# A longer written-out ring of gathers on GpSimd, and a wait ahead of its drain, in a masked-cumulative-sum kernel

## The chip, the cores and the metric

The kernel runs on one core of a Trainium2 chip. The metric is the device time of one execution in microseconds; a kernel's time is the median of several executions.

## What is computed

For each of 8 sequences the reference sums the rows of x from position 0 up to the middle of the sequence's length, and multiplies the sum by w:

```python
mask = (pos < lengths[:, None, None]).astype(np.float32)
cs = np.cumsum(x * mask, axis=1)
midpoints = (lengths // 2).clip(0)
mid_features = cs[b_idx, midpoints, :]
return np.matmul(mid_features[:, None, :], w).squeeze(1)
```

x is 8 x 8192 x 512 in float32, w is 512 x 512. Since the midpoint is always inside the length, only the rows 0 to length // 2 of each sequence matter. How many these are depends on the lengths, which are data.

## The kernel before

The kernel reads only the rows that count. It takes the sum as a matmul: rows of x stand on the 128 partitions, and a small matrix of zeros and ones (`ww`, one column for each sequence) is the stationary side, so PE adds up rows into `s_ps`.

Rows come in three ways. The rows 64 to 255 of each sequence (the front) are fetched by SP at once (L467). Rows beyond 256 are gathered by GpSimd: one indirect DMA brings 128 units of 8 rows (128 x 16 KB, 2 MB) into one of R = 3 slots of `xt` (`fetch`, L227 to L231). The first 64 rows of each sequence (`xb`) and w (`wt`) are fetched last, in plain DMAs of GpSimd, behind all gathers (L256 to L263). w comes in four pieces with a semaphore each, `s_w[0]` to `s_w[3]`.

The number of gathers is known only on the chip. DVE works it out and leaves it in `count`; each engine loads it into a register and loops. The order of the work is written out by hand, with semaphores:

- GpSimd makes three opening gathers (L236 to L248), then a ring of further ones. A turn of the ring waits for `s_now`, which tells that the indices of the slot have been written, issues the gather, and takes `s_now` down again (L250 to L252). When no gather is left it goes to `gp_end` (L255), issues the DMAs for xb and w, drains (L264), waits for both stores of the output (`s_out`, L265) and leaves.
- SP waits for each gather's landing (`s_full`) and for its weights (`s_wr`), and passes this on to PE as `s_rdy` (`relay`, L149).
- PE multiplies a slot's 8 rows of each partition (L395) and says `s_done`.
- ACT then copies the next indices to `now` (L185, which raises `s_now`) and the next weights to `ww` (L188).

At the end PE adds the xb rows into `d_ps`, combines both sums with a folding matrix (`mf_ps`, L446 and L449), and multiplies by the pieces of w (`o_ps`, L459); DVE and ACT copy the result out, and SP and ACT store a half each (L207).

The function `ring` (L123) writes the loop of an engine. Each turn has a compare that leaves the ring, the body, and a branch to the next turn; the last turn takes the turns off the register `left` and goes back to the first. It is used by SP, ACT and GpSimd, with as many turns written out as `xt` has slots.

Of the kernel before, what the change touches and what calls it, by code (L numbers as in the profile page):

```python
# [15 lines left out]
def kernel(  # L16
# [22 lines left out]
    R = 3  # L39
# [20 lines left out]
    def sem(name):  # L60
        return tc.alloc_semaphore(name)
# [46 lines left out]
    s_w = [sem(f"w{k}") for k in range(4)]  # L108
# [11 lines left out]
    def weights_by_rows(at, n):  # L120
        return ww[:, at * B:(at + n) * B].rearrange("p (u b) -> p u b", b=B)

    def ring(eng, name, left, body):  # L123
        for s in range(R):
            with nc.body(f"{name}_0_{s}", valid_engines=[eng.engine]):
                eng.br_cmp(left, s, f"{name}_1_{s}", f"{name}_end", "IS_GT")  # L126
            with nc.body(f"{name}_1_{s}", valid_engines=[eng.engine]):
                body(s)
                if s == R - 1:
                    eng.reg_sub(left, left, R)  # L130
                eng.br(f"{name}_0_{(s + 1) % R}")


    def sync(sp):
        left = sp.alloc_register("left_sp")
        full = sp.alloc_register("full_sp")
        have = sp.alloc_register("have_sp")
        sp.reg_mov(full, 16)
        sp.reg_mov(have, 1)
        sp.wait_ge(s_dve, marks["count"])  # L140
        sp.load(left, count[:])
        sp.wait_ge(s_dve, marks["front"])
        sp.wait_ge(s_zero, 3)
        for f in range(PARTS):
            sp.wait_ge(s_front[f], 16)
            sp.sem_inc(s_rdy, 1)
        sp.br("sy_0_0")

        def relay(s):  # L149
            sp.wait_ge(s_wr, have)  # L150
            sp.wait_ge(s_full[s], full)
            sp.sem_inc(s_rdy, 1)
            sp.reg_add(have, have, 1)
            if s == R - 1:
                sp.reg_add(full, full, 16)

        ring(sp, "sy", left, relay)
        with nc.body("sy_end", valid_engines=[sp.engine]):
            sp.wait_ge(s_dve, marks["out0"])
            sp.wait_ge(s_act, 3)  # L160
            store(sp, 0)
            sp.br(END)


    def scalar(act):
# [16 lines left out]
        def weigh(s):  # L182
# [7 lines left out]
            act.reg_add(turn, turn, 1)  # L190

        ring(act, "ac", left, weigh)
        with nc.body("ac_end", valid_engines=[act.engine]):
            act.wait_ge(s_pe, 2)
# [15 lines left out]
    def gpsimd(pool):  # L210
        pool.iota(v_i[:], pattern=[[P * U, C], [1, U]], base=HEAD, channel_multiplier=0)
        pool.iota(r_i[:, FU:], pattern=[[2, BU], [-(BU // 2), FB]], base=0,
                  channel_multiplier=BU // 2).then_inc(s_pool, 1)
        pool.wait_ge(s_pool, 1)
        for k in range(4):
            pool.iota(at_i[32 * k:32 * k + 32], pattern=[[P, C]],
                      base=64 * (k % 2) + 8 * (k // 2) + 63 * 8 * k,
                      channel_multiplier=16).then_inc(s_pool, 1)
        pool.tensor_scalar(out=row[:, 2 * B + 2:], in0=lens[:, ::2], scalar1=0.5, scalar2=0.25,
                           op0=ALU.mult, op1=ALU.add)._wait_ge(s_len, 16).then_inc(s_pool, 1)  # L220
        pool.wait_ge(s_pool, 6)
        pool.iota(r_i[:, :FU], pattern=[[2, FU], [-(FU // 2), FB]], base=2 * TOP,
                  channel_multiplier=FU // 2)
        pool.iota(fold_i[:], pattern=[[-32, 2], [-1, B]], base=P, channel_multiplier=1,
                  ).then_inc(s_pool, 1)

        def fetch(to, units, at, n, full):  # L227
            return pool.indirect_dma_start(  # L228
                out=to, out_offset=None, in_=units,
                in_offset=bass.IndirectOffsetOnAxis(ap=at, axis=0),  # L230
                bounds_check=n - 1, oob_is_err=False).then_inc(full, 16)  # L231

        left = pool.alloc_register("left_pool")
        pool.wait_ge(s_dve, marks["idx"])
        pool.br("gp_b_0")
        for c in range(R):  # L236
            if c > 0:
                with nc.body(f"gp_a_{c}", valid_engines=[pool.engine]):
                    pool.br_cmp(left, c, f"gp_b_{c}", "gp_end", "IS_GT")
            with nc.body(f"gp_b_{c}", valid_engines=[pool.engine]):  # L240
                got = fetch(xt[:, c], xu, now[:, c:c + 1], B * UB, s_full[c])
                if c > 0:
                    got._wait_ge(s_done, c)
                if c == 0:
                    pool.load(left, count[:])  # L245
                if c == R - 1:
                    pool.reg_sub(left, left, R)
                pool.br(f"gp_a_{c + 1}" if c + 1 < R else "gp_0_0")  # L248

        def gather(s):  # L250
            fetch(xt[:, s], xu, now[:, s:s + 1], B * UB, s_full[s])._wait_ge(s_now, 1)
            pool.sem_inc(s_now, -1)  # L252

        ring(pool, "gp", left, gather)
        with nc.body("gp_end", valid_engines=[pool.engine]):  # L255
            for f in range(PARTS):  # L256
                pool.dma_start(out=xb[:, f], in_=x[FB * f:FB * (f + 1), :TOP].rearrange(  # L257
                    "b (q u) d -> q b (u d)", u=BU)).then_inc(s_back[f], 16)
            pool.dma_start(out=wt[:, :2], in_=w[HALVES[0]].rearrange("(p k) d -> p k d", k=2),
                           ).then_inc(s_w[0], 16)  # L260
            pool.dma_start(out=wt[:, 2], in_=w[QUARTERS[2]]).then_inc(s_w[1], 16)
            for g, at in enumerate(HALVES):
                pool.dma_start(out=wt[:, 3, at], in_=w[QUARTERS[3], at]).then_inc(s_w[2 + g], 16)  # L263
            pool.drain()  # L264
            pool.wait_ge(s_out, 32)  # L265
            pool.br(END)
# [126 lines left out]
    def tensor(pe):  # L393
# [40 lines left out]
        with nc.body("pe_end", valid_engines=[pe.engine]):  # L434
# [17 lines left out]
            for k in range(KC):  # L452
# [10 lines left out]

    programs = [(nc.vector, vector, "dv"), (nc.sync, sync, "sy"), (nc.scalar, scalar, "ac"),
                (nc.gpsimd, gpsimd, "gp")]
    for f in range(PARTS):
        nc.sync.dma_start(out=xt[:, f + 1, :FU * D], in_=x[FB * f:FB * (f + 1), TOP:HEAD].rearrange(  # L467
            "b (q u) d -> q b (u d)", u=FU)).then_inc(s_front[f], 16)
    nc.scalar.dma_start(out=lens[:], in_=lens_words).then_inc(s_len, 16)
    left = nc.tensor.alloc_register("left_pe")  # L470
# [37 lines left out]
```

## Time and profile before

| what | value |
|---|---|
| median of 5 runs | 82.94 us (82.58 to 83.58) |
| the profiled execution, its own time | 82.64 us |
| its span, from the first to the last instruction | 80.5 us |
| mean granted TensorE clock | 0.992 |
| busy: PE / POOL / DVE / ACT | 59.3 / 19.9 / 11.8 / 9.7 us |
| read from HBM | 32.51 MB, 404 GB/s over the span |
| gathers | 13, each 4.9 us after the one before in the middle of the span, landing 11.8 us after its issue (median) |

Times in the profile are microseconds from the first instruction. PE is TensorE's matmuls, PEld its weight loads, DVE VectorE, ACT ScalarE, POOL GpSimd, SP SyncE; a "q" behind a name (POOLq, SPq) is the engine's sequencer, which does waits, branches, register work and drains, and isn't counted as busy. PE's busy time holds matmuls whose result isn't used (`idle`, L399), which fill its waits. "issue" in the chain is time in which the engine waited for nothing that the profile shows, here mostly a semaphore wait at the sequencer.

### The profile page before, as it was taken

What the parts mean: (1) busy time and instruction counts of PE and PEld (TensorE: products, weight loads), DVE (VectorE), ACT (ScalarE), POOL (GpSimd) and SP (SyncE); (2) the same over time, 40 slices, a digit from 0 to 9 for tenths busy, and PEclk for the clock granted to TensorE, in tenths of its full rate; (3) what the DMA queues carried; (4) which work ended last, traced back from release to release, by engine and by line L of the source; (5) the groups of instructions that cost most, each with busy time, mean ns of one, the idle gap of its engine ahead of it and who ended that gap; (6) DMA issues with size and microseconds to landing.
All of it is one profiled execution on the core that took longest, in us unless ns stands there. A gap on an engine that the chain in (4) does not pass through costs nothing.

```text
span 80.5 us, 1176 instructions
## 1 busy us (share of the span) xinstructions
PE 59.3 (74%) x360; PEld 14.1 (17%) x360; DVE 11.8 (15%) x43; ACT 9.7 (12%) x31; POOL 19.9 (25%) x32
## 2 busy tenths in 40 slices
PE   0599979996593967939489493975939679399940
PEld 0212202120110202112020110201102021112820
DVE  0799300990000000000000000000000000003130
ACT  2971000102010010201001020010100100000220
POOL 5432050844022040310404004040220793000000
PEclk9999999999999999999999999999999999999996
DMA  0899999999999999999999999999999999999700
GB/s 0 342 427 403 452 427 407 440 432 432 399 423 472 399 407 472 415 415 472 415 407 448 440 407 415 464 423 399 448 448 407 423 456 415 399 383 407 269 0 8
DMA packets 2803, 31.23 MB, mean 388 GB/s; under 512 B 434, under 2 KB 450, under 8 KB 962
## 3 DMA queue, kind: packets, MB, share of 16 engines
q0 software_dynamic: 2480, 28.05, 82.4%
q1 hardware_dynamic: 304, 3.15, 9.5%
q8 instruction: 1, 0.02, 0.1%
q10 hardware_dynamic: 18, 0.01, 0.0%
HBM read 32.51 MB, written 0.02 MB: 404 GB/s over the span
## 4 chain that ended last, share of the span: by engine, by line
issue 59%; POOL 14%; DMA 14%; PE 5%; DVE 2%; POOLq 2%; ACTq 0%; SPq 0%
POOL xt L228 14%; DMA xb<-in_x_dram 12%; DMA lens<-in_lengths_dram 1%; PE mf_ps L446 1%; PE o_ps L395 1%; PE d_ps L395 1%; PE bc_ps L408 1%; DVE o_sb L276 1%; POOL xb L257 1%; POOLq L245 1%; PE mf_ps L449 1%; POOLq L228 0%; DVE row L276 0%; POOLq L126 0%; DVE ge L276 0%
## 5 line engine op out<-in xcount | busy, mean ns | idle before, releaser
L395 PE MATMUL s_ps<-xt,ww 128*8 128x512 f32 x240 | 29.3, 594 | 15.0 <-PEq L415 15.0
L401 PE MATMUL idle_ps<-ones 128*4 128x512 f32 x58 | 29.2, 630 | 0.0
L228 POOL DMA_INDIRECT xt<-in_x_dram,now x13 | 14.8, 1135 | 45.9 <-POOLq L252 36.9
L395 PEld LDWEIGHTS s_ps<-xt,ww 128*8 128x8 f32 x240 | 5.8, 88 | 37.9 <-issue 37.8
L276 DVE COPY s_sb<-s_ps 128x256 f32<-128x256 f32 x2 | 0.8, 420 | 55.4 <-PE s_ps L395 55.4
L401 PEld LDWEIGHTS idle_ps<-ones 128*4 128x4 f32 x58 | 5.1, 90 | 20.4 <-issue 20.4
L185 ACT COPY now<-idx 128x1 int32 x10 | 1.9, 191 | 44.2 <-PE s_ps L395 44.2
L276 DVE TENSOR_TENSOR early<-v_f,ends 128x192 f32<-128x192 f32 (+1 forms) x2 | 2.4, 1192 | 5.4 <-PE s_ps L395 5.4
L408 PE MATMUL bc_ps<-row,ones 1*128 1x26 f32 x2 | 0.6, 398 | 2.9 <-DVE p L276 2.9
L188 ACT COPY ww<-wc 128x64 f32 x10 | 2.4, 244 | 0.1
L276 DVE TENSOR_TENSOR wc<-early,ge 128x192 f32<-128x192 f32 (+1 forms) x2 | 2.4, 1192 | 0.1
L166 ACT ACTIVATE xt<-xt 128x2048 uint32<-128x2048 uint32 x1 | 1.9, 1909 | 0.0
L196 ACT COPY d_sb<-d_ps 128x128 f32<-128x128 f32 x2 | 0.4, 269 | 12.1 <-PE d_ps L395 12.1
L178 ACT COPY ww<-wc 128x64 f32<-128x64 f32 x3 | 0.7, 244 | 8.1 <-PE s_ps L395 6.7
L166 ACT ACT_TABLE_LOAD x1 | 1.3, 1283 | 1.5 <-SPq L52 1.5
L395 PE MATMUL d_ps<-xb,ww 128*8 128x256 f32 x16 | 1.3, 388 | 0.1
L446 PE MATMUL mf_ps<-fold,s_sb 128*128 128x8 f32 x8 | 1.3, 265 | 0.0
L257 POOL DMA_DIRECT2D xb<-in_x_dram x2 | 1.2, 614 | 0.0
L263 POOL DMA_DIRECT2D wt<-in_w_dram x2 | 1.2, 647 | 0.0
L446 PEld LDWEIGHTS mf_ps<-fold,s_sb 128*128 128x128 f32 x8 | 1.1, 196 | 0.5 <-DVE s_sb L276 0.5
L395 PE MATMUL o_ps<-wt,mf_sb 128*8 128x128 f32 x32 | 1.1, 273 | 0.0
L408 PEld LDWEIGHTS bc_ps<-row,ones 1*128 1x128 f32 x2 | 0.5, 306 | 2.9 <-DVE p L276 2.9
(47 smaller groups left out, 14.1 us busy)
## 6 DMA issues: line engine op xcount, KB each, us to landing
xt<-in_x_dram SPq DMA_DIRECT2D x2, 1536.0 KB, 8.2
xb<-in_x_dram POOLq DMA_DIRECT2D x2, 512.0 KB, 9.4
wt<-in_w_dram POOLq DMA_DIRECT2D x1, 512.0 KB, 10.5
wt<-in_w_dram POOLq DMA_DIRECT2D x1, 256.0 KB, 10.7
wt<-in_w_dram POOLq DMA_DIRECT2D x2, 128.0 KB, 10.4
xt<-in_x_dram,now POOLq DMA_INDIRECT x13, 11.8
lens<-in_lengths_dram ACTq DMA_DIRECT2D x1, 0.1 KB
out_dram<-o_sb SPq DMA_DIRECT2D x1, 8.0 KB
```

What stands on the lines that cost most here:

```text
L166: act.memzero(xt[:, 1:, FU * D:]).then_inc(s_zero, 1)
L185: act.copy(out=now[:, s:s + 1], in_=idx[:, bass.ds(c, 1)]).then_inc(s_now, 1)
L188: act.copy(out=weights_of(s), in_=wc[:, bass.ds(c, 1)].rearrange("p c e -> p (c e)"),).then_inc(s_wr, 1)
L228: return pool.indirect_dma_start(out=to, out_offset=None, in_=units, in_offset=bass.IndirectOffsetOnAxis(ap=at, axis=0), bounds_check=n - ...
L245: pool.load(left, count[:])
L257: pool.dma_start(out=xb[:, f], in_=x[FB * f:FB * (f + 1), :TOP].rearrange("b (q u) d -> q b (u d)", u=BU)).then_inc(s_back[f], 16)
L263: pool.dma_start(out=wt[:, 3, at], in_=w[QUARTERS[3], at]).then_inc(s_w[2 + g], 16)
L276: do(*args, **kw).then_inc(s_dve, 1)
L395: return pe.matmul(to[32 * j:32 * j + weights.shape[1], :rows.shape[1]], lhsT=weights, rhs=rows, start=start, stop=False, skip_group_check ...
L401: pe.matmul(idle_ps[:FB], lhsT=ones[:, :FB], rhs=ones[:, :1].to_broadcast((P, D)), start=True, stop=True, skip_group_check=True)
L408: pe.matmul(bc_ps[:, :3 * B + 2], lhsT=ones[:1], rhs=row[:], start=True, stop=True,)._wait_ge(s_dve, marks["row"]).then_inc(s_pe, 1)
L446: pe.matmul(mf_ps[i][:, B * (k % 2):B * (k % 2 + 1)], lhsT=s_sb[:, QUARTERS[k]], rhs=fold[:], start=(k % 2 == 0), stop=False, skip_group_c ...
```

## The change

The ring gets a parameter for the number of turns that are written out. GpSimd's ring is written out for 2R = 6 turns; the slot of a turn is its number modulo 3. SP's and ACT's rings keep three turns. Behind the last DMA of w a wait for `s_w[3]`, the semaphore of w's last piece, is put ahead of the drain.

```diff
-    def ring(eng, name, left, body):
-        for s in range(R):
+    def ring(eng, name, left, body, turns=R):
+        for s in range(turns):
             with nc.body(f"{name}_0_{s}", valid_engines=[eng.engine]):
                 eng.br_cmp(left, s, f"{name}_1_{s}", f"{name}_end", "IS_GT")
             with nc.body(f"{name}_1_{s}", valid_engines=[eng.engine]):
-                body(s)
-                if s == R - 1:
-                    eng.reg_sub(left, left, R)
-                eng.br(f"{name}_0_{(s + 1) % R}")
+                body(s % R)
+                if s == turns - 1:
+                    eng.reg_sub(left, left, turns)
+                eng.br(f"{name}_0_{(s + 1) % turns}")
...
-        ring(pool, "gp", left, gather)
+        ring(pool, "gp", left, gather, 2 * R)
...
                 pool.dma_start(out=wt[:, 3, at], in_=w[QUARTERS[3], at]).then_inc(s_w[2 + g], 16)
+            pool.wait_ge(s_w[3], 16)
             pool.drain()
             pool.wait_ge(s_out, 32)
```

In the built program GpSimd has 84 instructions instead of 69. The wait for `s_w[3]` is carried by the drain itself. A plain turn's branch to the next turn falls away in both kernels, since the next turn follows it; only the last turn's branch, back to the first, is left.

## The prediction

> **What bounds the kernel now.** I read the page first (spans and slices), then the busy time by stage, then the chain that ended last, then the groups of single source lines of GpSimd. The slices of the page:
>
> ```profile
> span 80.5 us, 1176 instructions
> ...
> POOL 5432050844022040310404004040220793000000
> ...
> DMA  0899999999999999999999999999999999999700
> ```
>
> DMA is full from the second slice to slice 37, GpSimd (POOL) mostly idle. The busy time by stage (columns: window, its length, then busy time of PE, PEld, DVE, ACT, POOL, granted clock, DMA share, GB/s) says the same in numbers:
>
> ```profile
> 20.00:64.00 44.00, 32.39 (x180) 6.50 (x180) 0.00 (x0) 3.56 (x18) 9.07 (x10) 1.00 1.01 430
> 64.00:76.30 12.30, 9.97 (x84) 3.36 (x88) 0.93 (x3) 0.43 (x2) 3.12 (x6) 1.00 0.96 389
> 76.30:80.50 4.20, 0.99 (x32) 0.70 (x32) 0.74 (x3) 0.52 (x2) 0.00 (x0) 0.85 0.02 4
> ```
>
> From 20 to 64 us all 16 DMA engines are taken (share 1.01) at 430 GB/s, while GpSimd works 9.07 of 44 us. So the middle is set by bytes, not by who issues them. One gather of 2 MB takes 4.9 us at that rate, and the gathers follow each other at just 4.9 us. The end of the chain, in order of time (start, length, what):
>
> ```profile
> 62.81 0.98 POOL xt L228
> 63.79 0.56 POOL xb L257
> 64.36 9.77 DMA xb<-in_x_dram
> 74.12 0.04 issue
> 74.17 0.64 PE d_ps L395 x8
> ...
> 76.30 1.00 PE o_ps L395 x32
> 77.30 0.02 issue
> 77.32 0.28 DVE o_sb L276
> 77.60 0.03 issue
> 77.63 0.29 DVE o_sb L276
> ```
>
> The last piece of x (xb) lands at 74.1 because it stands behind the gathers; then PE, copies and the two stores follow. GpSimd's drain is not in it. Three lines of GpSimd alone (sequencer operation, count, ns min/median/max, first and last start):
>
> ```profile
> L264 POOLq DRAIN  x1: 11997/11997/11997, 65.6 to 65.6; - x1
> L266 POOLq COMPARE_BRANCH  x1: 42/42/42, 79.4 to 79.4; - x1
> L228 POOL DMA_INDIRECT xt<-in_x_dram,now x13: 984/984/2657, 5.3 to 62.8; - x13
> ```
>
> The drain runs from 65.6 to 77.6. GpSimd then waits for the two stores until 79.4. There are 13 gathers: 3 of the opening and 10 of the ring.
>
> **Part 1, the ring for six turns.** Ten ring gathers make three jumps back now (after turns 3, 6, 9) and one then (after turn 6). A jump turn shows what is saved. In the chain GpSimd's s_now decrement (L252) is at 28.32, then L130 and L131 (36 and 38 ns), the next compare, and the address move of the next gather (L228) at 28.70: 0.38 us. In a plain turn L252 is at 33.22 and the move at 33.37: 0.15 us. So a jump costs 0.23 us, two fewer save 0.46 us of sequencer time. None of it is on the path: the gather of the turn has already gone to the engine (28.55 in the jump turn, 0.23 us after L252; 18.67 after 18.44 in a plain turn, the same 0.23), and after the bookkeeping the sequencer waits 4.49 us for the next index ("28.73 4.49 issue"). That wait is the cover; a delay longer than it would still have to outlast the transfers queued in front. A gather lands 11.8 us after its issue, of which 4.9 are its own bytes, about 1.0 its issue (984 ns) and about 1.2 the latency of a small transfer (that of lens, in the chain): 11.8 - 4.9 - 1.0 - 1.2 = 4.7 us may be lost before the DMA engines run dry. Value taken: 0. What it adds is 15 instructions (69 to 84 on GpSimd by the instruction order): code that may cross a block. That is the rival below.
>
> [...] The row of this trace:
>
> ```profile
> q8 instruction: 1, 0.02, 0.1%
> ```
>
> One block was fetched in the whole execution: 0.1% of 16 engines' 80.5 us, about 1.3 us of one DMA engine (its packet in the trace: from 75.9, 1.1 us). The row doesn't tell whose it is. At 75.9 PE starts on its last stretch (o_ps), and PE's code is the longest by far (its matmuls are written out), so I take it as PE's, which this change leaves where it is. By the row the change costs 0. [...]
>
> **Part 2, the drain waits for the last piece of w.** Queued behind it on GpSimd are only the drain, the wait for both stores and the final branch; the transfers of xb and w are all issued before it, so SP's and ACT's queues and every transfer keep their times. The last w piece is issued at 66.5 and lands 10.3 us later, at about 76.8. Then the drain runs. [...] How long is it if it starts at 76.8? From below: other drains of this trace take nothing that a view lists as busy, so 0. From above: 77.6 less the end of the last issue (65.95 + 1.18 = 67.1), 10.4 us, if its time were fixed. It ended 0.8 us after the last landing, so I take it as waiting for the transfers, with 0.8 us left: end at 77.6 as before. Cover: until 79.4 GpSimd would wait for the stores anyway, so up to 79.4 - 76.8 = 2.6 us cost nothing. Value taken: 0. A gain is bounded too: nothing waits for the drain but the end of the program, which the stores set.
>
> **Sum.** 0 + 0 against the profiled execution: 82.64 us, span 80.5 and 2.1 around it. The median of the five runs, 82.94, is 0.3 above; the forecast for the median is 82.9.
>
> **Rivals.**
> 1. A code block boundary falls into the ring (slower). GpSimd stops after a gather until a block has come. If the block's fetch stands behind the gathers already queued, it comes after about 11.8 + 1.1 = 12.9 us from that gather's issue. The next gather would have been issued 4.9 us after it, so it is 8.0 late; 4.7 of it are covered by the queue, 3.3 are idle DMA: 82.9 + 3.3 = 86.2. It decides from 4.7 us of lateness on; a fetch that overtakes the data (1.1 us) is hidden in the 3.9 us for which GpSimd is idle in each turn. For it: GpSimd's drain ends 0.5 us after that one fetched block, so the block might be GpSimd's, asked for at 65.6 and queued behind data for 10 us. Against: no gather of the trace shows such a gap, and an execution of only 84 instructions needn't cross a block.
> 2. The drain has work of its own per transfer that now starts late (slower). The third gather's issue took 2.66 us against 0.98; if those 1.7 us are the clearing of old transfers and several are due at the drain, it takes 3.5 to 5 us and ends at 80.3 to 81.8, 0.9 to 2.4 us after 79.4: 83.8 to 85.3. With the fixed 10.4 us it would be 82.9 + 7.8 = 90.7. Against: it ended soon after the last landing.
> 3. The fetched block is GpSimd's and leaves the tail (faster). It holds one DMA engine for 1.1 us among the last pieces. Where it stands in front of xb or w, all of PE's end waits: at most 82.9 - 1.1 = 81.8. Against: here o_ps starts at 76.2 and runs 1.06 us without a gap, so the block cost nothing.
> 4. It does nothing that can be seen: the forecast itself.
>
> **How the numbers follow.** No effect 0.50 (82.3 to 83.5, own range); rival 1 0.17 (85.5 to 88); rival 2 0.13 (83.8 to 85.3, little beyond); rival 3 0.20 (81.8 to 82.1). 1% (0.83 us) is about what a measurement of this kernel can tell from no change. So faster 0.20, within 1% 0.50, slower 0.30. The range leaves out the most of rival 3 and the upper half of rival 1: 82.0 to 86.5.
>
> **What would show it.** Part 1 right: gathers still every 4.9 us, DMA share 1.00 from 20 to 64 us, L131 on GpSimd once instead of three times. Part 2 right: a drain of 0.1 to 0.8 us at about 76.8, the last branch of GpSimd still at 79.4. Wrong: one gather issued 8 us late and a slice with DMA below 9 (rival 1); the final branch right behind a long drain (rival 2); the instruction packet moved and xb or o_ps earlier (rival 3).

## The result, and the profile after

The changed kernel takes 83.09 us (median of 42 executions), the one before 83.02 (79 executions). The ratio is 1.0014, its 95% interval 1.0003 to 1.0024: slower by about 0.12 us. That is inside the range of 82.3 to 83.5 us given for "no effect", but it is a small loss and not nothing. The profiled execution took 83.23 us, with a span of 81.1.

What part 1 promised is there. The busy time by stage of the changed kernel, with the columns as before:

```profile
20.00:64.00 44.00, 32.39 (x180) 6.51 (x180) 0.00 (x0) 3.56 (x18) 8.93 (x10) 1.00 1.01 429
```

DMA is as full as before (share 1.01 in both), and GpSimd makes one jump back in its ring instead of three (the source line of the jump, one row for each sequencer; before, GpSimd's row has x3):

```profile
L131 SPq COMPARE_BRANCH  x4: 37/38/38, 26.0 to 70.0; - x4
L131 ACTq COMPARE_BRANCH  x3: 38/38/38, 28.5 to 57.8; - x3
L131 POOLq COMPARE_BRANCH  x1: 38/38/38, 43.3 to 43.3; - x1
```

The chain that ended last takes the same steps with the same lengths:

```profile
64.50 9.78 DMA xb<-in_x_dram
74.28 0.04 issue
74.33 0.64 PE d_ps L396 x8
...
77.48 0.28 DVE o_sb L277
77.75 0.03 issue
77.79 0.29 DVE o_sb L277
```

xb takes 9.78 us to land against 9.77, and from its landing to the last copy there are 3.80 us in both. The chain ends there, but the span doesn't. Behind it stands the closing barrier, in which GpSimd releases the other engines (their steps start 0.04 to 0.06 us after its second semaphore step, at 79.84 to 79.86 us before and at 80.38 to 80.40 after), and it shows only when its source line is asked for. First the kernel before, then the one after (operation, count, ns, start of the first and the last):

```profile
L503 POOLq DRAIN  x3: 34/47/103, 79.6 to 80.2; - x3
L503 SPq EVENT_SEMAPHORE  x2: 17/17/17, 79.8 to 80.4; - x2
```

```profile
L504 POOLq DRAIN  x3: 34/40/146, 79.8 to 80.8; - x3
L504 SPq EVENT_SEMAPHORE  x2: 17/17/17, 80.4 to 81.0; - x2
```

Before, SP passes the barrier 0.2 us after GpSimd's first drain in it; after, 0.6 us. In the instruction records the place is a single step of GpSimd: its two semaphore steps behind that drain start 0.08 us apart before (79.72 and 79.80) and 0.46 us apart after (79.88 and 80.34). The other engines' own drains in the barrier take what they took (SP's 7 ns, ACT's and PE's 8, DVE's 10, in both). (The two profiled spans differ by 0.59 us. About 0.17 of it is there already when GpSimd's last wait ends, 79.36 us before and 79.53 after; since the mean spans below differ by 0.38, I take this part as scatter.) The DMA queues of the changed kernel have a row more than those of the kernel before:

```profile
q8 instruction: 1, 0.02, 0.1%
q14 instruction: 1, 0.01, 0.0%
```

The new packet is 8192 bytes of code, at 81.02 us, 0.7 us after the stalled step. The 16 KB on q8 is still there, at 76.0 us. GpSimd's drain ahead of the barrier, which now waits for w, and the branch behind it, which waits for the stores:

```profile
L265 POOLq DRAIN  x1: 1624/1624/1624, 76.9 to 76.9; - x1
```

```profile
L267 POOLq COMPARE_BRANCH  x1: 43/43/43, 79.5 to 79.5; - x1
```

The drain runs from 76.9 to 78.5, and the branch that waits for the stores is still the later one.

So two numbers have to be put together: a step in the span that costs 0.38 us more, and a time that grew by only 0.12.

### The profile page after: what moved, and what is told of

Read it like the earlier page. It is cut to its first block, busy times and chain, and to the rows that moved or that the text cites. A ratio compares the mean times of both kernels' runs of the same rounds, so it can differ in the third digit from the quotient of the medians.

```text
span 81.1 us, 1172 instructions
## 1 busy us (share of the span) xinstructions
PE 59.7 (74%) x360; PEld 14.1 (17%) x360; DVE 11.8 (15%) x43; ACT 9.7 (12%) x31; POOL 19.9 (25%) x32
## 4 chain that ended last, share of the span: by engine, by line
issue 57%; POOL 16%; DMA 14%; PE 5%; DVE 2%; POOLq 2%; ACTq 0%; SPq 0%
POOL xt L228 16%; DMA xb<-in_x_dram 12%; DMA lens<-in_lengths_dram 1%; PE mf_ps L447 1%; PE o_ps L396 1%; PE d_ps L396 1%; PE bc_ps L409 1%; DVE o_sb L277 1%; POOL xb L257 1%; POOLq L245 1%; PE mf_ps L450 1%; POOLq L228 0%; POOLq L126 0%; DVE row L277 0%; DVE z L277 0%
## 5 line engine op out<-in xcount | busy, mean ns | idle before, releaser
L228 POOL DMA_INDIRECT xt<-in_x_dram,now x13 | 14.7, 1134 | 46.1 <-POOLq L252 37.1
## 6 DMA issues: line engine op xcount, KB each, us to landing
wt<-in_w_dram POOLq DMA_DIRECT2D x1, 512.0 KB, 10.5
wt<-in_w_dram POOLq DMA_DIRECT2D x2, 128.0 KB, 10.4
```

What stands on the lines that cost most here:

```text
L228: return pool.indirect_dma_start(out=to, out_offset=None, in_=units, in_offset=bass.IndirectOffsetOnAxis(ap=at, axis=0), bounds_check=n - ...
```

## The experiments

In all of them "outside" is the time of an execution less its span. The kernel before ran 150 times beside the experiments, and its executions fall into two groups: in 130 outside is 2.33 to 2.66 us (median 2.52), in the other 20 it is 2.09 to 2.19 (median 2.15), with nothing between (spans are on record to 0.1 us). The spans of the two groups are the same (mean 80.60 and 80.58); the times differ as outside does (median 83.07 and 82.72). The profiled execution of before, with 82.64 and 80.5, belongs to the small group. In all 44 recorded executions of the changed kernel outside is 2.0 to 2.2.

The new packet above has 8192 bytes, and I take it as a block of GpSimd's code. The runs below look for the place where GpSimd passes from one block to the next, the code border. It follows from the stalls and from a count of the entries (places) of GpSimd's compiled code. Left out of the count are the branch labels, and the second of the two entries that each gather has there; the traces have no record of it. (It is not the count of 69 and 84 given with the change.) Counted so, the code has 62 places before and 74 after, and the border is behind the 68th. That is 6 places behind the end of the kernel before, and exactly between the two stalled semaphore steps of the kernel after.

That the second entries take no place is inferred: only so does one border fit the stalls of the changed kernel, e1, e7 and e8. The expectations below count otherwise: e1 to e4 with the labels (134 places in the changed kernel, border behind the 128th, which is again 6 places ahead of its end), e5 to e8 without them but with the second entries (68 and 83 places, border behind the 77th). The latter gives the same border wherever all nine gathers of the changed kernel stand ahead of it, and comes too late in e3 and e8.

Three theories stand in the expectations of e1 to e4: that GpSimd's code border makes the gap of 0.46 us in the closing barrier (code-block), that the drain makes it, which starts only after the last landing (drain), and that the kernels are equal and the two profiled executions scatter (chance).

| kernel | where GpSimd's code border lies | us, median | span | outside |
|---|---|---|---|---|
| before (150) | 6 places behind the kernel's end | 83.05 | 80.55 | 2.50 |
| after (44) | in the closing barrier | 83.09 | 80.9 | 2.14 |
| e1, ring alone | in the closing barrier | 83.14 | 81.0 | 2.14 |
| e2, drain's wait alone | as before | 83.17 | 80.65 | 2.48 |
| e3, 19 places more | among the last six transfers, ahead of the drain | 82.98 | 80.8 | 2.14 |
| e4, 26 more | ahead of the first xb transfer | 82.96 | 80.8 | 2.15 |
| e5, 66 more at the start | ahead of the first iota | 82.77 | 80.6 | 2.17 |
| e6, e10, after and 4 more | behind the drain, which waits for w | 82.70, 82.72 | 80.55, 80.6 | 2.13 |
| e7, after and 3 more | behind the branch that waits for the stores | 83.07 | 80.9 | 2.15 |
| e8, 33 more at the start | in the ring, behind its first turn | 82.87 | 80.7 | 2.13 |
| e9, after and 66 more at the start | ahead of the first iota | 82.77 | 80.6 | 2.14 |

**e1, the ring alone.**

```diff
-            pool.wait_ge(s_w[3], 16)
             pool.drain()
```

> The six-turn ring alone, the drain without its wait. [...] Drain theory (the drain that starts only after the last landing is what costs): no loss, 83.0. Chance theory (the kernels are equal and the two profiled executions differ by scatter): 83.0 and no gap in the closing barrier.

83.14 us, ratio 1.0001 (0.9985 to 1.0016). The two semaphore steps start at 79.79 and 80.25: the gap of 0.46 us is there without the drain's wait, as the code-block theory has it. The drain theory is out as the cause of the gap.

**e2, the drain's wait alone,** in the kernel before.

> The ring of three turns, the drain with its wait for the last piece of w: 113 places of code. Code-block theory: no gap in the closing barrier (0.08 us), 83.0 us or a little below. Drain theory: the drain takes 1.6 us from the last landing as in the changed kernel, and the time is 83.1. It also shows if the late drain gains anything that the code border then takes back: in that case below 82.9.

83.17 us, ratio 0.9998 (0.9977 to 1.0019). The steps are 0.08 us apart, and the drain takes 1.62 us from 76.8: no loss from it, and no gain. The surprise is outside: its profiled execution has a span of 80.5 and a time of 82.94, so 2.4 us stand outside, and its code packet comes at 82.8 us, when its last instruction is long done. That suggested what the runs after it were made for: the border costs this kernel too, only later.

**e3, the kernel before with GpSimd's code made longer,** by places that are jumped over.

```diff
         with nc.body("gp_end", valid_engines=[pool.engine]):
+            pool.br_cmp(left, 1 << 20, "gp_pad", "gp_go", "IS_GT")
+        with nc.body("gp_pad", valid_engines=[pool.engine]):
+            for _ in range(18):
+                pool.sem_inc(s_zero, 1)
+        with nc.body("gp_go", valid_engines=[pool.engine]):
             for f in range(PARTS):
```

> The kernel before with one compare that is run (about 0.1 us, beside 4 us of waiting) and 18 semaphore steps with two labels that are jumped over, ahead of the last transfers: GpSimd's code is 134 places long, as in the changed kernel, with three turns and no wait at the drain. Code-block theory: the same gap of 0.46 us at the same step of the closing barrier, 83.1 us or a little more. Drain and chance theories: 83.0, no gap.

82.98 us, ratio 0.9992 (0.9974 to 1.0010), and no gap in the barrier. The expectation was a miss: it counted labels as places. Without them and without the gathers' second entries e3 has 81 places against 74 of the changed kernel, not as many, and the border lies behind the fourth of the last six transfers. The trace agrees that it is ahead of the drain: the drain starts 3.28 us after the end of the compare at 62.79 us; in the kernel before it starts 2.87 us after the end of the branch that leaves the ring. So about 0.41 us are lost on the sequencer among the transfers. But the six transfers start at the same distances as in the kernel before, so the loss is hidden. What the run shows is a third way to pay. The code packet (8192 bytes) comes at 68.8 us, in the middle of the last data, and holds its DMA engine for 0.32 us; xb takes 0.29 us longer to land:

```profile
64.32 10.06 DMA xb<-in_x_dram
```

10.06 us instead of 9.77, and the span is 0.25 longer than that of before, while outside is 2.14 and not 2.50.

**e4, 26 places more** (25 semaphore steps in the same edit).

> The same with 25 semaphore steps that are jumped over: 141 places, the border of 128 falls on the drain itself, which runs from 65.6 to 77.6 us beside 12 us of other engines' work. Code-block theory: the crossing is hidden, no gap in the closing barrier, 83.0 us. If the border costs only because of the length of the code and not where it is passed: 83.1 like the other padded kernel.

82.96 us, ratio 0.9987 (0.9970 to 1.0004), no gap in the barrier, the packet at 67.2 us. By the count above the border lies in the places that are jumped over, ahead of the first xb transfer, and not on the drain. The drain starts 0.32 us late by the same measure as in e3. Hidden as expected, but as in e3 not for nothing: the span is 80.8.

**e5, the border at the start.** 66 places ahead of GpSimd's first iota, 64 of them jumped over.

```diff
+        skip = pool.alloc_register("skip_pool")
+        pool.reg_mov(skip, 0)
+        pool.br_cmp(skip, 1, "gp_pad", "gp_go", "IS_GT")
+        with nc.body("gp_pad", valid_engines=[pool.engine]):
+            for _ in range(64):
+                pool.sem_inc(s_zero, 1)
+        with nc.body("gp_go", valid_engines=[pool.engine]):
+            begin(pool)
```

> The kernel before, with a register set, a compare and 64 semaphore steps that are jumped over ahead of GpSimd's first iota, so that the border of its code (behind its 77th instruction, labels not counted) is passed in the first microsecond, while the DMA engines are still idle. Border theory as it now stands: the kernels before and after both pay some 0.4 us for this border, the one before behind the span (2.5 us between time and span instead of 2.1), the one after inside the closing barrier. Here it is paid where GpSimd is not on the path: span 80.5 us, 2.1 around it, 82.6 us, below both. Rival (the 2.5 around the span has nothing to do with the border): 83.0. Rival (the stall of 0.4 us in GpSimd's iotas delays the index chain and the first gather): up to 83.0 with the first gather issued 0.3 later.

82.77 us, ratio 0.9978 (0.9961 to 0.9994). Outside is 2.17 in the median and above 2.35 in none of 14 executions, with the span of the kernel before. GpSimd's timeline shows where the border is paid now (start, length, then the idle time before it):

```profile
1.59 0.42 POOL L211 IOTA v_i<- 128x248 int32 x1 [1.14 <-SPq L52]
...
5.71 1.23 POOL L228 DMA_INDIRECT xt<-in_x_dram,now  x1 [2.08 <-DVE r_f L286]
```

The first iota starts at 1.59 us instead of 1.07. Of these 0.52 us 0.23 are the added move and branch (with the same edit and fewer places, in e6 and e8, it starts at 1.30), and 0.29 are the border. The first gather starts at 5.71 instead of 5.28; the front transfers still fill the DMA engines then (busy for nine tenths or more from 4 to 6 us), and nothing comes later for it: xb lands at 74.20, against 74.12 and 74.28. The packet of code comes at 2.1 us.

**e6, the changed kernel with four places more at its start** (the same edit with 2 semaphore steps).

> The changed kernel with four more places at GpSimd's start: the border lies just behind the drain, which waits for the last piece of w. If the next code block is asked for only when the drain starts to run (76.9 us), its 8 KB come behind all data and the stall is hidden in the wait for the stores: span 80.5, 82.6 us. If the sequencer asks for it while the drain still waits for its semaphore, the 8 KB come at about 69 us as in the kernel padded by 21, in front of xb on one DMA engine: span 80.8, 82.97.

82.70 us, ratio 0.9979 (0.9953 to 1.0004); run again as e10. The time is that of the first case. The packet comes at 79.6 us, behind all data and 1.1 us after the drain's end at 78.5; in the changed kernel too it comes 1.1 us after the last instruction ahead of the border. So I take the crossing as what sets it off, and the stall as lying between the drain's end and the branch that waits for the stores, 78.5 to 79.5 us. xb takes what it took before, and the branch and the barrier stand where they stood:

```profile
64.43 9.77 DMA xb<-in_x_dram
```

```profile
L514 POOLq DRAIN  x3: 34/40/103, 79.7 to 80.3; - x3
L514 SPq EVENT_SEMAPHORE  x2: 17/17/17, 79.9 to 80.5; - x2
```

Whether the drain's wait has a part in this is not shown: no run has the border right behind a drain that doesn't wait.

**e7, the changed kernel with three places more.**

> The changed kernel with three more places: the border lies behind the branch that waits for the two stores. The block would be asked for at about 78.5 or at 79.5 us, behind all data. If it is asked for while the branch waits: hidden, span 80.5, 82.6 us. If only when the branch has run: 0.4 us in the path, 83.1.

83.07 us, ratio 1.0014 (0.9995 to 1.0033), span 80.9. The last case: the branch that waits for the stores and the instruction behind it are 0.45 us apart (79.44 and 79.89) instead of 0.18, a stall of 0.28. One place decides between 82.7 and 83.07.

**e8, the border in the ring.** 33 places at the start of the kernel before.

> The kernel before with 33 more places at its start: the border lies in the ring of three turns, behind the semaphore step of the second turn, so that it is passed three times forward and three times back. Border theory with blocks that stay: each pass 0.4 us, hidden in the 4.5 us for which GpSimd waits in a turn; one or more fetches of 8 KB among the gathers, each 0.3 us on one DMA engine: span 80.8, 83.0 us. If the jump back needs a block that is gone: a stall of several us in the third turn, a gather issued late, 84 to 95.

82.87 us, ratio 0.9993 (0.9974 to 1.0011). GpSimd's chain at the first pass over the border, in the turn after it, and around a jump back and the next pass:

```profile
18.67 0.03 POOLq L252
18.70 0.20 issue
18.90 0.26 POOL xt L228
19.16 0.04 issue
19.20 0.03 POOLq L228
...
23.55 0.02 POOLq L252
23.57 0.07 issue
23.63 0.03 POOLq L126
23.67 0.03 issue
23.70 0.03 POOLq L228
...
28.61 0.03 POOLq L130
28.64 0.03 issue
28.67 0.04 POOLq L131
28.71 0.03 issue
28.74 0.23 POOL xt L228
...
33.41 0.02 POOLq L252
33.43 0.16 issue
33.59 0.03 POOLq L126
```

The first crossing stalls GpSimd like that in the barrier: from L252 to the address move of the next gather (L228) it takes 0.53 us, against 0.15 in the next turn, 0.38 more. Later crossings are cheaper: forward, L126 comes 0.18 us after L252 (0.08 elsewhere), and a jump back is about 0.1 us longer than in the kernel before (0.49 us from L252 to the address move, against 0.38). All of it is hidden in the turn's wait: the next gathers start at 23.77, 28.74 and 33.64 us, against 23.71, 28.55 and 33.45 in the kernel before, and the last at 63.01 against 62.81. The stall stands behind the first turn of the ring and not behind the second: the expectation had the place wrong by one turn. There is one packet of code, at 22.3 us, 3.6 us after the first crossing begins, and none for the later crossings, forward or back. The several us that were expected for a jump back to a block that is gone didn't come, and no gather is issued late by more than the 0.2 us above.

**e9, the changed kernel with the border at the start.**

> The changed kernel, six turns and the drain's wait, with the 66 places of the early border at GpSimd's start. Border theory: with the border out of the way the two parts of the change cost nothing by themselves, 82.7 to 82.8 like the kernel before with an early border, span 80.6 and 2.15 around it. Rival (the longer ring or the later drain cost something of their own): 82.9 or more at a time of 2.15 around the span.

82.77 us, ratio 0.9970 (0.9952 to 0.9988), the same as e5. With the border out of the way the ring of six turns and the drain's wait cost nothing that these runs can tell, and bring nothing.

**e10, e6 once more.**

> The changed kernel with four more places once more, for a closer interval: 82.7, ratio to the kernel before 0.997 to 0.998 with an interval that leaves out 1.

82.72 us, ratio 0.9970 (0.9956 to 0.9985). The interval leaves out 1: the changed kernel with four more places is faster than the kernel before, by about 0.25 us.

## Why the prediction was wrong

**Part 1, the ring.** The saving of two jumps is hidden, as worked out: the ring turns take place 4.9 us apart and the jump line shows x1. The step that failed is "Value taken: 0. What it adds is 15 instructions", priced at nothing by the row of the one fetched block ("By the row the change costs 0"). The added instructions take 12 places (four in each of three turns) and move the end of GpSimd's code from 6 places ahead of a code border to 6 places behind it, so that the border falls into the closing barrier. There it stalls the barrier by 0.38 us. And the border had been paid before: 0.36 us outside the span, in 130 of 150 executions. The term that was missing is therefore a difference of two: + 0.38 in the span (80.60 to 80.98 in the mean) and - 0.33 outside (mean 2.46 to 2.13), which leaves 0.05, against a measured 0.07 between the medians and 0.12 by the ratio. The first part is shown by e1, the second by e5 and e9, in which both are gone. That the two nearly cancel is luck: nothing in the prediction weighed one against the other.

That the page of before gave no hint of it has a reason that can be seen: the profiled execution was one of the few without the cost outside, and the sum was made against it, "span 80.5 and 2.1 around it". The median stood 0.3 above it, and the prediction gave no reason for that. It was the border: without it the 20 executions of the small group have a median of 82.72, with it the other 130 have 83.07.

**The one fetched block.** "The row doesn't tell whose it is" holds, and the packet was rightly not taken for GpSimd's: the 16 KB on q8 is at 75.9 to 76.2 us in every kernel here, wherever GpSimd's border lies (that it is PE's stays argued). But it was the wrong row to price the change by, and "One block was fetched in the whole execution" is a misreading, since the row counts the span alone. The trace of before has seven packets of 8192 bytes on q14 ahead of its first instruction (10.5 to 7.5 us ahead), and none behind its last; this execution was one without the cost outside. That of e2, which paid it, has one at 82.8 us, behind its span. That an execution of 84 instructions needn't cross a block was an argument that no row showed; by the count above the changed kernel passes a border behind its 68th place.

**Rival 1** had the right cause, a code border, with the wrong place and price. It put the border into the ring at 3.3 us, from a stop until a block has come behind the queued gathers. No run shows such a stop, nor the 3.3 us. e8 put the border there: 0.38 us at the first crossing and 0.1 at each later one, hidden in the turn's wait. GpSimd runs on behind the border at 19.2 us, 3 us before the packet comes at 22.3, so it didn't wait for that packet; what the packet holds is not shown. What costs is the crossing itself (0.28 to 0.38 us more where nothing else is waited for: e7, e1 and the changed kernel) and, in the stream of data, the 0.32 us for which the packet holds a DMA engine (e3).

**Part 2, the drain.** "The transfers keep their times" holds (xb 9.77 and 9.78 us), and so does the cover. The size was off: the drain was given 0 to 0.8 us from 76.8, and takes 1.62, because its end in the kernel before, 0.8 us after the last landing, was read as all that is left. It leaves 1.0 of the 2.6 us of cover. (The upper bound of 10.4 us is 10.5 by the figures given for it; nothing hangs on that.) Of **rival 2** the 3.5 to 5 us didn't come. **Rival 3** is out with q8.

**Chances.** The time lies within 1%, as the likeliest case said; the small loss came from a code border, which rival 1 named.

## What to carry to other kernels

Where the last tenths count, ask for the instruction rows of the DMA queues and for the lines behind the end of the chain, and compare time less span over many executions: here a cost that the span didn't hold moved into it (0.38 us more in the span, 0.33 less outside), and the span of one profile told a change that the time didn't. Writing the ring out for six turns moved GpSimd's later code by 12 places, across a border. The place at which the border falls could be chosen by a few places more: four at GpSimd's start (e6, two of them jumped over) put it where the engine waits and no data queue behind it. This was worth 0.2 to 0.3 us, and the edit that was meant for something else 0.1 us of loss.

## What the runs showed of the hardware that was not expected

- GpSimd's code border stalls its sequencer when it is passed for the first time: 0.38 us in the closing barrier (the changed kernel, e1) and in the ring (e8), 0.28 us ahead of the barrier (e7), 0.29 us at the start (e5). Passed again in the ring it costs about 0.1 us, forward or back. One border fits these stalls only with the branch labels left out of the count: e3, which counted with them is as long as the changed kernel, has no gap in the closing barrier.
- A packet of 8192 bytes follows the first crossing. It comes 1.0 to 1.1 us after the last instruction ahead of the border when the DMA engines have no data left (the changed kernel, e1, e6, e7, e10), and 3.6 to 4.0 us after it among data (e8, e4). Among data it isn't as late as the data themselves (9.8 us for xb): in e3 it comes at 68.8 us, and xb lands at 74.4.
- Why the kernel before escapes the cost outside its span in 20 of 150 executions stays open, and so does what the packet of 8192 bytes holds.
- A drain of GpSimd that starts after all its transfers have landed takes 1.62 us (from 76.9 us in the changed kernel, from 76.8 in e2 and e6).
